# Gate and up blocks by seven products: 19 of 22 instead of 10, two of the weight sums made by adding transfers, the feed-forward in three parts

## The chip, the cores and the metric

The kernel runs on one core of a Trainium2 chip. The metric is the device time of one execution in microseconds; for a run of several executions it is the median. The core has a matrix engine (PE, whose weight loads are listed as PEld), a vector engine (DVE), an activation engine (ACT), a general engine (POOL) and a sequencer that mostly issues transfers (SP). Each works through its own queue in order, and they wait for each other by semaphores. DMA engines move data between main memory and the on-chip memory; matmul results stand in the banks of PSUM.

## The reference

Two layers of an encoder over 512 positions of width 1024, in float32. Each layer mixes three branches (attention, convolution, neighbourhood attention), then comes the part that matters here, the feed-forward with 2816 hidden channels, and then a gated input embedding:

```python
h = rmsnorm(x, norm_ffn[i])
x = x + (jax.nn.silu(h @ w_ffn_gate[i]) * (h @ w_ffn_up[i])) @ w_ffn_down[i]
h = rmsnorm(x, norm_ple[i])
x = x + jax.nn.sigmoid(h @ w_ple_gate[i]) * (p[i] @ w_ple_in[i])
```

`w_ffn_gate` and `w_ffn_up` are 1024 x 2816, `w_ffn_down` is 2816 x 1024.

## The kernel before

**Tiles.** Channels lie along the 128 partitions and the 512 positions along the free dimension. x is eight tiles of 128 x 512 (`x[0]` to `x[7]`), the hidden channels are 22 blocks of 128 (`NFB`). float32 precision comes from three matmuls per product (`mm3`, L174): each operand is split into a high half, which PE takes at its rounded precision, and a low half that holds the rest, and high x high, high x low and low x high are added. `split` (L161) makes the halves: ACT copies the high one (L142), DVE subtracts it for the low one (L156). `weights` (L165) loads a block of weights of up to 1024 columns into `wr` by a transfer from SP (L170) and splits it into `wh` and `wl`; there are three buffers of each. It does so under a raised priority, up to `w_ahead` = 400 steps ahead of the place where the products stand.

**Order.** PE's order is the program's order (`manual_schedule`); for the other engines a scheduler places the instructions by priority and dependency, and each then runs its queue in that order.

**Feed-forward (`ffn`, L1012).** The hidden blocks are worked in two halves of eleven (`HB`). For each block the products with gate and up are made, giving a tile g = silu(gate) * up, whose halves stand in `md`; after eleven blocks the down products follow: eight output tiles, each a sum over eleven blocks, whose weights come as 1024 and 384 columns. The result is multiplied by the norm's row factor `rb` and added to x (L1055, L1056).

**Plain blocks** make gate and up by `gemm`: eight chunks of the width by three matmuls of 512 columns each, twice, 48 matmuls.

**Blocks by seven products** (`SEVEN`, L52: ten of the 22, every second from 3 on; `seven`, L938) treat gate and up together as a 2 x 2 arrangement of blocks. The weights are a11, a12 (gate, first and second half of the width) and a21, a22 (up); the activations are b11, b12, b21, b22 (halves of the width by halves of the positions). Instead of eight block products there are seven of sums of the blocks (Strassen and Winograd's scheme): four of weights (s1 to s4) and four of activations (t1 to t4, made once per layer by `quarters`, L909). Each block product is four chunks by three matmuls of 256 columns, so 84 matmuls of half the width. Per block SP loads gate and up (two loads of 512 KB, L944, L945), DVE makes s1 to s4 (L960 to L964, into a `qk` buffer of 2048 columns, of which there are two), and ACT and DVE split [a11 a12], a22, [s1 s3] and [s2 s4]. The products go to three banks A, C and Q; three intermediate results are copied out by ACT (p1, p4, p5; L985 to L989) before more is added in the same place, and DVE joins the results by seven operations of 256 columns (L995 to L1001). Then silu (ACT), times up (DVE), and the split into `md`.

Two consecutive seven-product blocks would use different banks by the count `n`; with every second block plain they use `sc`, `sc`, `av`, and the plain ones `mm`.

The norms of `main_norm` (L247) take two short PE steps and a power on POOL (L221) and run beside the first products of the stage that follows; `pair` (L193) makes two outputs at once, all chunks but the last for both and then the last for both, so that the last activation may come late.

Of the kernel before, what the change touches and what calls it, by code (L numbers as in the profile page):

```python
# [12 lines left out]
F32R = mybir.dt.float32r  # L13
# [23 lines left out]
PLE = 256  # L37
DFF = 2816
NFB = DFF // P
HB = NFB // 2  # L40
EPS = 1e-6
OFF_QA, OFF_KA, OFF_VA, OFF_GLU = 0, 512, 1024, 1536
OFF_QC, OFF_KC, OFF_VC, OFF_G = 2560, 3072, 3584, 4096
# [5 lines left out]
BG = dict(glu=2, natten=1, values=3, diff=1, gatec=2, branchc=2, gateb=4, mergea=4, mergea2=2)  # L49
FIRST = (["v"] * 4 + ["pt"] * 2 + ["y", "b"], ["y"] * 5 + ["pt"] * 2 + ["b"])  # L50
EARLY = 6
SEVEN = (3, 5, 7, 9, 11, 13, 15, 17, 19, 21)  # L52
GAP = 144
BACC = dict(dynamic_dma_scratch_size=1024)

# [5 lines left out]
class Net:  # L61
# [131 lines left out]
    def pair(self, outs, aps, acts):  # L193


        ws = [self.weights(ap, 1024) for ap in aps]
        n = len(acts)
        for ks in (range(n - 1), (n - 1,)):
            for out, (wh, wl) in zip(outs, ws):
                for k in ks:  # L200
                    s = slice(k * P, (k + 1) * P)
                    self.mm3(out, wh[:, s], wl[:, s], *self.halves(acts[k]), k == 0, k == n - 1)
                    self.chunk()
# [705 lines left out]
    def quarters(self, x, h, j):  # L909


        one, two = slice(0, 256), slice(256, 512)
        g = lambda k: self.par(self.i, "ffn", k)
        f = []
        for k in (j, j + 4):
            v = self.sb("t", [P, 512])
            self.act(v, x[k], AF.Copy, scale=g(k))
            f.append(v)
        b11, b12, b21, b22 = f[0][:, one], f[0][:, two], f[1][:, one], f[1][:, two]
        u = self.sb("t", [P, 2, 256])  # L920
# [12 lines left out]
        ha, hb = self.halves(h[j]), self.halves(h[j + 4])  # L933
        cut = lambda p, c: (p[0][:, c], p[1][:, c])
        return dict(b11=cut(ha, one), b21=cut(hb, one), b22=cut(hb, two),
                    **{f"t{n + 1}": (o[:, 0], o[:, 1]) for n, o in enumerate(d)})

    def seven(self, wg, wu, bs, n):  # L938


        nc = self.nc
        with self.tc.high_priority(offset=min(self.w_ahead, self.tc.cur_priority - self.p0)):
            g, u = self.sb("wr", [P, 1024]), self.sb("wr", [P, 1024])
            nc.sync.dma_start(g, wg)  # L944
            nc.sync.dma_start(u, wu)  # L945
# [12 lines left out]
            s = self.sb("qk", [P, 2048])  # L958
            s1, s3, s2, s4 = (s[:, q * 512:q * 512 + 512] for q in range(4))
            self.tt(s1, a21, a22, ALU.add)  # L960
            self.tt(s3, a11, a21, ALU.subtract)
            halve(*wide(), s[:, :1024], ("s1", "s3"))
            self.tt(s2, s1, a11, ALU.subtract)
            self.tt(s4, a12, s2, ALU.subtract)  # L964
            halve(*wide(), s[:, 1024:], ("s2", "s4"))
        tags = ("mm", "mm", "mm") if n % 2 else ("sc", "sc", "av")
        A, C, Q = (self.ps(t, (P, 2, 256)) for t in tags)

        def product(out, w, b, first):
            wh, wl = ws[w]  # L970
            mm = nc.tensor.matmul
            for k in range(4):
                c = slice(k * P, k * P + P)
                bh, bl = bs[k][b]
                mm(out, wh[:, c], bh, start=first and k == 0, stop=False, skip_group_check=True)  # L975
# [19 lines left out]
        self.tt(p5, p5, p4, ALU.subtract)  # L995
        self.tt(gg[:, 0], A[:, 0], rb[:, 0], ALU.mult)
        self.tt(p1, p1, A[:, 1], ALU.add)
        self.tt(uu[:, 0], p1, Q[:, 0], ALU.add)
        self.tt(uu[:, 1], uu[:, 0], p5, ALU.add)
        self.tt(gg[:, 1], p1, C[:, 0], ALU.add)  # L1000
# [11 lines left out]
    def ffn(self, h, x):  # L1012
        self.phase = "ffn"
        i = self.i
        self.halfs, count = 0, 0
        st, hn, bs = [], [], self.four
        for half in range(2):
            mids = []
            for f in range(HB):
                fb = half * HB + f  # L1020
                md = self.sb((["z"] * 5 + ["y"] * 5 + ["pt"])[f], [P, 2, 512], F32R)
                mids.append(md)
                wg, wu = self.a["w_fg"][i, fb], self.a["w_fu"][i, fb]
                if fb in SEVEN:
                    count = (count + 1) % 2 if fb - 1 in SEVEN else 0
                    g = self.seven(wg, wu, bs, count)
                    self.split(md[:, 0, :], md[:, 1, :], g)
                    continue
                g = self.sb("t", [P, 512])
                pg, pu = self.ps("mm"), self.ps("mm")  # L1030
# [12 lines left out]

                def up(pu=pu, g=g, md=md):
                    self.tt(g, g, pu, ALU.mult)
                    self.split(md[:, 0, :], md[:, 1, :], g)

                self.ready(up)
                if fb in (0, 1):
                    self.four.append(self.quarters(x, h, 2 + fb))  # L1050
            for m in range(KD):
                ps = self.ps("mm")
                self.gemm(ps, self.a["w_fd"][i, half, m], mids)
                d = self.sb("t", [P, 512])
                self.tt(d, ps, self.rb, ALU.mult)  # L1055
                self.tt(x[m], x[m], d, ALU.add)  # L1056
                if half:
                    if m in (0, 2):
                        two = self.parts_of("qk", [2, 512], 2, F32R)
                    hn.append(self.norm_chunk(m, x[m], self.par(i, "ple", m),  # L1060
                                              two[m % 2] if m < 4 else "v", st))
        self.main_norm(st[0])
        return hn

# [256 lines left out]
def _layout(v):  # L1321
# [4 lines left out]
    for i in range(L):  # L1326
# [7 lines left out]
    down = f["w_ffn_down"].reshape(L, 2, HB * P, D)  # L1334
    return {
        "xT": np.ascontiguousarray(f["x"][0][n].T).reshape(KD, P, S),
        "pT": np.ascontiguousarray(f["p"][:, 0][:, n].transpose(0, 2, 1)).reshape(L, 2, P, S),
# [15 lines left out]
        "w_fd": _blocks(down),  # L1353
        "w_pi": _blocks(f["w_ple_in"]),
        "w_pg": _blocks(f["w_ple_gate"]),
    }
# [15 lines left out]
```

## Time and profile before

| | |
|---|---|
| median of 3 runs | 1801.97 us (1801.7 to 1802.68) |
| the profiled execution | 1802.28 us, of which 1800.3 us are the span from its first to its last instruction |
| PE busy | 1790.7 us (99%), 9346 matmuls |
| PEld busy | 1535.5 us (85%) |
| DVE busy | 1315.5 us (73%) |
| ACT busy | 846.9 us (47%) |
| POOL busy | 24.6 us (1%) |
| moved by DMA | 221.30 MB, a mean of 123 GB/s |
| mean granted PE clock | 0.999 |

How to read the lines: in the page, a group of instructions stands as line, engine, operation, output<-inputs, shapes and count, then busy time, the mean of one in ns, the idle time of the engine just before them and who ended it. In a timeline a row is start, duration (both in us), engine, line, operation, tiles. Start to start of two rows in a row is the pitch; durations overlap, since the engines begin an instruction before the previous one has written its last result. A row of DMA issues ends with the size in KB and the median time in us from issue to landing. L numbers of the profile are those of the kernel before.

### The profile page before, as it was taken

To read this page: it belongs to the slowest core of one execution; us is meant where nothing else is said; L and a number is where in the kernel's file an instruction comes from. 1 tells how busy PE (TensorE), PEld (TensorE's weight loads), DVE (VectorE), ACT (ScalarE), POOL (GpSimd) and SP (SyncE) were. 2 spreads that over 40 slices of the span, in tenths; PEclk is the share of its full clock that TensorE was granted. 3 is DMA by queue.
4 is the path that set the end of the run, shared out by engine and by line. 5 is a ranking of instruction groups with operands and counts; after the bars stand their busy time and mean duration, and the time that the engine had idled before them with its cause. 6 is when DMAs were issued, how large, how long until landed. Compare 5 with 4: busy or idle time off the path is not lost.

```text
span 1800.3 us, 25007 instructions
## 1 busy us (share of the span) xinstructions
PE 1790.7 (99%) x9346; PEld 1535.5 (85%) x9346; DVE 1315.5 (73%) x2198; ACT 846.9 (47%) x1457; POOL 24.6 (1%) x58
## 2 busy tenths in 40 slices
PE   9999999999999999999999999999999999999998
PEld 7888888888889889988888888888888898899887
DVE  7877888987767547665776788889886764577556
ACT  5577545325454324444535765552355543244444
POOL 0000000000000000000000000000000000000000
PEclk9999999999999999999999999999999999999999
DMA  5665531334423232233446655322253232333332
GB/s 205 193 179 167 159 111 54 103 105 148 142 83 110 84 123 94 94 110 126 143 140 202 169 160 149 98 76 96 92 192 112 96 104 75 101 110 102 103 115 94
DMA packets 90313, 221.30 MB, mean 123 GB/s; under 512 B 11984, under 2 KB 20688, under 8 KB 90192
## 3 DMA queue, kind: packets, MB, share of 16 engines
q1 hardware_dynamic: 89472, 218.39, 38.6%
q8 instruction: 74, 1.21, 0.3%
q10 hardware_dynamic: 720, 1.31, 0.2%
q14 instruction: 47, 0.39, 0.1%
HBM read 180.86 MB, written 7.34 MB: 105 GB/s over the span
## 4 chain that ended last, share of the span: by engine, by line
PE 96%; ACT 1%; DVE 1%; issue 0%; DMA 0%; POOLq 0%; DVEq 0%; ACTq 0%
PE ffn_mm L176 9%; PE ffn_mm L178 9%; PE ffn_mm L177 9%; PE ffn_sc L977 3%; PE ffn_sc L976 3%; PE ffn_sc L975 3%; PE mergea_mm L176 2%; PE mergea_mm L178 2%; PE mergea_mm L177 2%; PE diff_sc L783 2%; PE gatec_mm L176 2%; PE gatec_mm L177 2%; PE gatec_mm L178 2%; PE gateb_mm L178 2%; PE gateb_mm L177 2%; PE gateb_mm L176 2%
## 5 line engine op out<-in xcount | busy, mean ns | idle before, releaser
L142 ACT ACTIVATE ffn_wh<-ffn_wr 128x1024 fp32r<-128x1024 f32 (+1 forms) x132 | 122.7, 931 | 233.0 <-PE ffn_mm L177 126.2
L156 DVE TENSOR_TENSOR ffn_wl<-ffn_wr,ffn_wh 128x1024 fp32r<-128x1024 f32 (+1 forms) x132 | 139.7, 1061 | 119.7 <-ACT ffn_wh L142 119.7
L159 DVE SCALAR_TENSOR_TENSOR conv_z<-glu_z,pre_par,conv_z 128x512 f32<-128x512 f32 x240 | 179.7, 749 | 3.3
L176 PE MATMUL ffn_mm<-wo_h,ffn_wh 128*128 128x512 f32 x384 | 150.0, 391 | 0.0
L177 PE MATMUL ffn_mm<-wo_h,ffn_wh 128*128 128x512 f32 x384 | 149.6, 390 | 0.0
L178 PE MATMUL ffn_mm<-wo_h,ffn_wl 128*128 128x512 f32 x384 | 149.5, 389 | 0.0
L178 PEld LDWEIGHTS ffn_mm<-wo_h,ffn_wl 128*128 128x128 f32 x384 | 72.1, 188 | 15.2
L176 PEld LDWEIGHTS ffn_mm<-wo_h,ffn_wh 128*128 128x128 f32 x384 | 72.2, 188 | 14.3
L177 PEld LDWEIGHTS ffn_mm<-wo_h,ffn_wh 128*128 128x128 f32 x384 | 72.2, 188 | 14.2
L142 ACT ACTIVATE mergea_wh<-mergea_wr 128x1024 fp32r<-128x1024 f32 (+1 forms) x32 | 27.1, 846 | 96.8 <-PE mergea_mm L177 79.6
L142 ACT ACTIVATE ffn_wh<-ffn_qk 128x1024 fp32r<-128x1024 f32 x40 | 42.1, 1053 | 59.9 <-PE ffn_mm L177 59.9
L977 PE MATMUL ffn_sc<-wo_h,ffn_wl 128*128 128x256 f32 x240 | 67.9, 283 | 0.0
L976 PE MATMUL ffn_sc<-wo_h,ffn_wh 128*128 128x256 f32 x240 | 67.9, 283 | 0.0
L975 PE MATMUL ffn_sc<-wo_h,ffn_wh 128*128 128x256 f32 x240 | 67.8, 283 | 0.0
L176 PE MATMUL ffn_mm<-ffn_z,ffn_wh 128*128 128x512 f32 x160 | 62.3, 389 | 0.0
L177 PE MATMUL ffn_mm<-ffn_z,ffn_wh 128*128 128x512 f32 x160 | 62.3, 389 | 0.0
L178 PE MATMUL ffn_mm<-ffn_z,ffn_wl 128*128 128x512 f32 x160 | 62.2, 389 | 0.0
L176 PE MATMUL ffn_mm<-ffn_y,ffn_wh 128*128 128x512 f32 x160 | 62.2, 389 | 0.0
L177 PE MATMUL ffn_mm<-ffn_y,ffn_wh 128*128 128x512 f32 x160 | 62.2, 389 | 0.0
L178 PE MATMUL ffn_mm<-ffn_y,ffn_wl 128*128 128x512 f32 x160 | 62.2, 389 | 0.0
L156 DVE TENSOR_TENSOR ffn_t<-ffn_mm,wo_r 128x512 f32<-128x512 f32 x56 | 38.6, 689 | 29.3 <-PE ffn_mm L178 29.2
L142 ACT ACTIVATE ffn_t<-ffn_t 128x512 f32<-128x512 f32 x44 | 27.6, 626 | 59.3 <-DVE ffn_t L156 59.0
(727 smaller groups left out, 5502.4 us busy)
## 6 DMA issues: line engine op xcount, KB each, us to landing
ffn_wr<-w_fg SPq DMA_DIRECT2D x44, 512.0 KB, 4.5
ffn_wr<-w_fu SPq DMA_DIRECT2D x44, 512.0 KB, 3.5
ffn_wr<-w_fd SPq DMA_DIRECT2D x32, 512.0 KB, 3.4
natten_wr<-w_in SPq DMA_DIRECT2D x16, 512.0 KB, 4.2
natten_b<-bias SPq DMA_DIRECT2D x32, 256.0 KB, 3.9
diff_wr<-w_in SPq DMA_DIRECT2D x16, 512.0 KB, 3.9
gatec_wr<-w_in SPq DMA_DIRECT2D x16, 512.0 KB, 3.9
gateb_wr<-w_in SPq DMA_DIRECT2D x16, 512.0 KB, 3.5
```

Of the source, the lines that this page charges most:

```text
L142: i = self.nc.scalar.activation(out, in_, func, **kw)
L156: return self.nc.vector.tensor_tensor(out, a, b, op)
L159: return self.nc.vector.scalar_tensor_tensor(out, a, s, b, op0, op1)
L176: mm(out, wh, ah, start=first, stop=False)
L177: mm(out, wh, al, start=False, stop=False)
L178: mm(out, wl, ah, start=False, stop=last)
L783: self.nc.tensor.matmul(out, st4[:, u, qs], st[:, ks], start=n == 0, stop=n == 1)
L975: mm(out, wh[:, c], bh, start=first and k == 0, stop=False, skip_group_check=True)
L976: mm(out, wh[:, c], bl, start=False, stop=False, skip_group_check=True)
L977: mm(out, wl[:, c], bh, start=False, stop=k == 3, skip_group_check=True)
```

## The change

- `SEVEN` is 3 to 21: nineteen of the 22 blocks. Plain ones are 0, 1 and 2.
- The feed-forward is worked in three parts of eight, seven and seven blocks (`PARTS`), each followed by its down products over its blocks, so x is added to three times. The down weights are no longer cut in halves on the host; a part takes its columns (1024, 896, 896). The first two down products of each part are made by `pair`.
- The scheme's signs are turned so that all weight sums are additions: s1 = a11 + a21, s2 = a22 + a21, s3 = s1 + a22, s4 = s3 + a12. s1 and s2 are made without DVE: SP loads a11 and a22 into the `qk` buffer, and POOL issues two transfers that add a21 from main memory to them (`accum_op`). a22 has a load of its own into `r`. So SP issues four loads per block (256, 256, 512 and 256 KB) and POOL two of 256 KB. DVE makes s3 and s4 only.
- The split of [s3 s4] has its own two pairs of buffers, `y` for even and `pt` for odd blocks, and `wh`/`wl` serve [a11 a12] and [s1 s2]. The result tiles `md` stand in `z` and three of `y`.
- Banks alternate by the number of the block: even ones (the plain ones too) use `mm`, odd ones `sc`, `sc`, `av`.
- silu, the product with up and the split of a block are put off (`pending`) until the next block's p5 has been copied (`flush`), and `behind` orders an instruction after another without a wait; at the start of the second and third part s3 of the first two blocks is ordered behind the last result's split.

```diff
-HB = NFB // 2
+PARTS = (range(0, 8), range(8, 15), range(15, 22))
-SEVEN = (3, 5, 7, 9, 11, 13, 15, 17, 19, 21)
+SEVEN = tuple(range(3, 22))
@@ pair
-        ws = [self.weights(ap, 1024) for ap in aps]
+        ws = [self.weights(ap, n * P) for ap in aps]
@@ quarters
-        self.tt(t1, b12, b11, ALU.subtract)
-        self.tt(t2, b22, t1, ALU.subtract)
+        self.tt(t1, b11, b12, ALU.subtract)
+        self.tt(t2, b22, t1, ALU.add)
         self.tt(t3, b22, b12, ALU.subtract)
-        self.tt(t4, b21, t2, ALU.subtract)
+        self.tt(t4, t2, b21, ALU.subtract)
@@ seven
-    def seven(self, wg, wu, bs, n):
+    def seven(self, wg, wu, bs, tags, spare, md, first):
-            g, u = self.sb("wr", [P, 1024]), self.sb("wr", [P, 1024])
+            lo, up = slice(0, 512), slice(512, 1024)
+            g, a22 = self.sb("wr", [P, 1024]), self.sb("r", [P, 512])
+            s = self.sb("qk", [P, 2048])
+            s1, s2, s3, s4 = (s[:, q * 512:q * 512 + 512] for q in range(4))
+            nc.sync.dma_start(s1, wg[:, lo])
+            nc.sync.dma_start(s2, wu[:, up])
             nc.sync.dma_start(g, wg)
-            nc.sync.dma_start(u, wu)
-            a11, a12, a21, a22 = g[:, :512], g[:, 512:], u[:, :512], u[:, 512:]
+            nc.sync.dma_start(a22, wu[:, up])
+            for q in (s1, s2):
+                nc.gpsimd.dma_start(q, wu[:, lo], accum_op=ALU.add)
...
             halve(self.sb("kh", [P, 512], F32R), self.sb("a", [P, 512], F32R), a22, ("a22",))
-            s = self.sb("qk", [P, 2048])
-            s1, s3, s2, s4 = (s[:, q * 512:q * 512 + 512] for q in range(4))
-            self.tt(s1, a21, a22, ALU.add)
-            self.tt(s3, a11, a21, ALU.subtract)
-            halve(*wide(), s[:, :1024], ("s1", "s3"))
-            self.tt(s2, s1, a11, ALU.subtract)
-            self.tt(s4, a12, s2, ALU.subtract)
-            halve(*wide(), s[:, 1024:], ("s2", "s4"))
-        tags = ("mm", "mm", "mm") if n % 2 else ("sc", "sc", "av")
+            halve(*wide(), s[:, :1024], ("s1", "s2"))
+            i = self.tt(s3, s1, a22, ALU.add)
+            if first:
+                self.behind(i, self.held)
+            self.tt(s4, s3, g[:, up], ALU.add)
+            halve(*spare, s[:, 1024:], ("s3", "s4"))
...
-        product(C[:, 0], "s1", "t1", True)
-        self.act(p5, C[:, 0], AF.Copy)
+        product(C[:, 0], "s2", "t1", True)
+        self.flush(self.act(p5, C[:, 0], AF.Copy))
         product(A[:, 0], "a12", "b21", False)
-        product(Q[:, 0], "s3", "t3", False)
-        product(A[:, 1], "s2", "t2", True)
+        product(Q[:, 0], "s1", "t3", False)
+        product(A[:, 1], "s3", "t2", True)
         product(C[:, 0], "s4", "b22", False)
...
-        self.act(gg, gg, AF.Silu, table="silu")
-        self.tt(gg, gg, uu, ALU.mult)
-        return gg.rearrange("p a b -> p (a b)")
+        def rest(then):
+            i = self.act(gg, gg, AF.Silu, table="silu")
+            if then is not None:
+                self.behind(i, then)
+            self.tt(gg, gg, uu, ALU.mult)
+            self.held = self.split(md[:, 0, :], md[:, 1, :], gg.rearrange("p a b -> p (a b)"))
+        self.pending.append(rest)
+    def behind(self, i, then):
+        self.tc.add_manual_dep(
+            i.ins, then.ins.name,
+            mybir.DependencyInfo(mybir.DependencyClass.NoSync, mybir.DependencyReason.DATA),
+            reason="order",
+        )
+    def flush(self, then=None):
+        while self.pending:
+            self.pending.pop(0)(then)
@@ ffn
-        for half in range(2):
+        spare = [[self.sb(t, [P, 1024], F32R) for _ in range(2)] for t in ("y", "pt")]
+        for part in PARTS:
             mids = []
-            for f in range(HB):
-                fb = half * HB + f
-                md = self.sb((["z"] * 5 + ["y"] * 5 + ["pt"])[f], [P, 2, 512], F32R)
+            for f, fb in enumerate(part):
+                tags = (("mm", "mm", "mm"), ("sc", "sc", "av"))[fb % 2]
+                md = self.sb("z" if f < 5 else "y", [P, 2, 512], F32R)
...
-                    count = (count + 1) % 2 if fb - 1 in SEVEN else 0
-                    g = self.seven(wg, wu, bs, count)
-                    self.split(md[:, 0, :], md[:, 1, :], g)
+                    self.seven(wg, wu, bs, tags, spare[fb % 2], md, part[0] and f < 2)
                     continue
...
+            self.flush()
+            down = [self.a["w_fd"][i, m][:, part[0] * P:(part[-1] + 1) * P] for m in range(KD)]
+            two = [self.ps(("mm", "sc")[fb % 2 == 0]) for _ in range(2)]
+            self.pair(two, down[:2], mids)
             for m in range(KD):
-                ps = self.ps("mm")
-                self.gemm(ps, self.a["w_fd"][i, half, m], mids)
+                if m < 2:
+                    ps = two[m]
+                else:
+                    ps = self.ps("mm")
+                    self.gemm(ps, down[m], mids)
...
-                if half:
+                if part is PARTS[-1]:
```

More of the change, by code (lines that the diff above doesn't have):

```diff
@@ L987, in seven @@
         self.act(p4, Q[:, 0], AF.Copy)
-        product(C[:, 0], "s1", "t1", True)
-        self.act(p5, C[:, 0], AF.Copy)
+        product(C[:, 0], "s2", "t1", True)
+        self.flush(self.act(p5, C[:, 0], AF.Copy))
         product(A[:, 0], "a12", "b21", False)
-        product(Q[:, 0], "s3", "t3", False)
-        product(A[:, 1], "s2", "t2", True)
+        product(Q[:, 0], "s1", "t3", False)
+        product(A[:, 1], "s3", "t2", True)
         product(C[:, 0], "s4", "b22", False)
         rb = self.rb.rearrange("p (a b) -> p a b", a=2)
-        self.tt(p5, p5, p4, ALU.subtract)
+        self.tt(p5, p4, p5, ALU.subtract)
         self.tt(gg[:, 0], A[:, 0], rb[:, 0], ALU.mult)
-        self.tt(p1, p1, A[:, 1], ALU.add)
-        self.tt(uu[:, 0], p1, Q[:, 0], ALU.add)
+        self.tt(p1, A[:, 1], p1, ALU.subtract)
+        self.tt(uu[:, 0], p1, Q[:, 0], ALU.subtract)
         self.tt(uu[:, 1], uu[:, 0], p5, ALU.add)
-        self.tt(gg[:, 1], p1, C[:, 0], ALU.add)
+        self.tt(gg[:, 1], C[:, 0], p1, ALU.subtract)
         self.tt(gg[:, 1], gg[:, 1], rb[:, 1], ALU.mult)
-        self.act(gg, gg, AF.Silu, table="silu")
-        self.tt(gg, gg, uu, ALU.mult)
-        return gg.rearrange("p a b -> p (a b)")
+        def rest(then):
[14 more added lines that the diff above has]
+            self.pending.pop(0)(then)
     def chunk2(self):
@@ L1014, in ffn @@
         i = self.i
-        self.halfs, count = 0, 0
+        self.halfs, self.pending = 0, []
         st, hn, bs = [], [], self.four
-        for half in range(2):
+        spare = [[self.sb(t, [P, 1024], F32R) for _ in range(2)] for t in ("y", "pt")]
+        for part in PARTS:
             mids = []
-            for f in range(HB):
-                fb = half * HB + f
-                md = self.sb((["z"] * 5 + ["y"] * 5 + ["pt"])[f], [P, 2, 512], F32R)
+            for f, fb in enumerate(part):
+                tags = (("mm", "mm", "mm"), ("sc", "sc", "av"))[fb % 2]
+                md = self.sb("z" if f < 5 else "y", [P, 2, 512], F32R)
                 mids.append(md)
@@ L1024, in ffn @@
                 if fb in SEVEN:
-                    count = (count + 1) % 2 if fb - 1 in SEVEN else 0
-                    g = self.seven(wg, wu, bs, count)
-                    self.split(md[:, 0, :], md[:, 1, :], g)
+                    self.seven(wg, wu, bs, tags, spare[fb % 2], md, part[0] and f < 2)
                     continue
                 g = self.sb("t", [P, 512])
-                pg, pu = self.ps("mm"), self.ps("mm")
+                pg, pu = (self.ps(t) for t in tags[:2])
                 if fb == 0:
@@ L1050, in ffn @@
                     self.four.append(self.quarters(x, h, 2 + fb))
+            self.flush()
+            down = [self.a["w_fd"][i, m][:, part[0] * P:(part[-1] + 1) * P] for m in range(KD)]
+            two = [self.ps(("mm", "sc")[fb % 2 == 0]) for _ in range(2)]
+            self.pair(two, down[:2], mids)
             for m in range(KD):
[L1052 to L1053 removed]
+                if m < 2:
[3 more added lines that the diff above has]
+                    self.gemm(ps, down[m], mids)
                 d = self.sb("t", [P, 512])
@@ L1056, in ffn @@
                 self.tt(x[m], x[m], d, ALU.add)
-                if half:
+                if part is PARTS[-1]:
                     if m in (0, 2):
-                        two = self.parts_of("qk", [2, 512], 2, F32R)
+                        qk = self.parts_of("qk", [2, 512], 2, F32R)
                     hn.append(self.norm_chunk(m, x[m], self.par(i, "ple", m),
-                                              two[m % 2] if m < 4 else "v", st))
+                                              qk[m % 2] if m < 4 else "v", st))
         self.main_norm(st[0])
@@ L1333, in _layout @@
     w_0 = _first(w_in[0])
-    down = f["w_ffn_down"].reshape(L, 2, HB * P, D)
     return {
@@ L1352, in _layout @@
         "w_fu": _blocks(f["w_ffn_up"]),
-        "w_fd": _blocks(down),
+        "w_fd": _blocks(f["w_ffn_down"]),
         "w_pi": _blocks(f["w_ple_in"]),
```

## The prediction

> **What bounds the kernel now.** I read the page first: busy shares, slices, chain.
>
> ```profile
> span 1800.3 us, 25007 instructions
> ...
> PE 1790.7 (99%) x9346; PEld 1535.5 (85%) x9346; DVE 1315.5 (73%) x2198; ACT 846.9 (47%) x1457; POOL 24.6 (1%) x58
> ...
> PE   9999999999999999999999999999999999999998
> ...
> PEclk9999999999999999999999999999999999999999
> ...
> PE 96%; ACT 1%; DVE 1%; issue 0%; DMA 0%; POOLq 0%; DVEq 0%; ACTq 0%
> ```
>
> TensorE works 1790.7 of 1800.3 us at full clock, and the chain that ended last is 96% PE. Then the stretches of the feed-forward, the only place that the change touches (columns: PE, PEld, DVE, ACT, POOL busy, clock, DMA share, GB/s):
>
> ```profile
> 550.00:600.00 50.00, 50.00 (x324) 45.83 (x323) 32.18 (x49) 21.07 (x31) 0.00 (x0) 1.00 0.26 87
> ...
> 700.00:800.00 100.00, 100.00 (x625) 90.71 (x624) 68.09 (x104) 43.40 (x62) 0.00 (x0) 1.00 0.33 104
> ```
>
> PE has no gap, DVE is at 64 to 68%, DMA at a third. So only fewer or shorter matmuls help here, and they help in full until another engine or a transfer makes PE wait.
>
> **What one more block by seven products saves.** From the timeline of PE: the first matmul of a seven-product block, of the plain block after it, and of the next two.
>
> ```profile
> 531.28 0.28 PE L975 MATMUL ffn_sc<-wo_h,ffn_wh 128*128 128x256 f32 x1
> ...
> 541.35 0.40 PE L176 MATMUL ffn_mm<-wo_h,ffn_wh 128*128 128x512 f32 x1
> ...
> 552.26 0.28 PE L975 MATMUL ffn_sc<-wo_h,ffn_wh 128*128 128x256 f32 x1
> ...
> 562.33 0.40 PE L176 MATMUL ffn_mm<-wo_h,ffn_wh 128*128 128x512 f32 x1
> ```
>
> A seven-product block (84 matmuls of 256 columns) takes 541.35 - 531.28 = 10.07 us, 0.12 each; a plain one (48 of 512 columns) 552.26 - 541.35 = 10.91. The listed durations (0.28, 0.40) overlap, so pitches count. The change converts nine blocks in each of two layers: 18 x (10.91 - 10.07) = 15.1 us off PE, the only gain. The down products keep their 22 x 8 x 3 matmuls per layer.
>
> **DVE in a run of seven-product blocks.** Before, plain and seven-product blocks alternate; now five, seven and seven stand in a row. DVE's pitches, one row of each width and its successor:
>
> ```profile
> 542.29 0.42 DVE L156 TENSOR_TENSOR ffn_t<-ffn_t,ffn_a 128x256 f32<-128x256 f32 x1
> 542.62 1.22 DVE L156 TENSOR_TENSOR ffn_wl<-ffn_wr,ffn_wh 128x1024 fp32r<-128x1024 f32 x1
> 543.76 0.69 DVE L156 TENSOR_TENSOR ffn_a<-ffn_wr,ffn_kh 128x512 fp32r<-128x512 f32 x1
> 544.36 0.69 DVE L156 TENSOR_TENSOR ffn_qk<-ffn_wr 128x512 f32<-128x512 f32 x1
> 544.96 0.69 DVE L156 TENSOR_TENSOR ffn_qk<-ffn_wr,ffn_wr 128x512 f32<-128x512 f32 x1
> ```
>
> 256 columns 0.33, 1024 columns 1.14, 512 columns 0.60 us. A new block gives DVE three low halves of 1024 (g, s1s2, s3s4), five operations of 512 (low a22, s3, s4, gate x up, low half of the result) and seven of 256: 3.42 + 3.00 + 2.31 = 8.7 us, of PE's 10.07: 87%. With all four sums left on DVE it would be 9.9. So DVE's throughput holds, but its cover shrinks from a third of the time to 1.3 us a block.
>
> **The two sums by transfers.** s1 and s2 now come from an SP load (256 KB) and, when that has landed, a POOL transfer that adds the other 256 KB. Per block SP issues four loads where it issued two (0.33 us each), POOL two. Both must be done before DVE adds a22 to s1 (s3; the first suffices) and ACT splits s1s2. The trace has no POOL transfer at all:
>
> ```profile
> q1 hardware_dynamic: 89472, 218.39, 38.6%
> q8 instruction: 74, 1.21, 0.3%
> q10 hardware_dynamic: 720, 1.31, 0.2%
> q14 instruction: 47, 0.39, 0.1%
> ...
> ffn_wr<-w_fu SPq DMA_DIRECT2D x44, 512.0 KB, 3.5
> ...
> mergea_wr<-w_br_a SPq DMA_DIRECT2D x16, 256.0 KB, 2.5
> ...
> pre_x<-xT SPq DMA_DIRECT2D x7, 256.0 KB, 5.0
> ...
> diff_r<-rope SPq DMA_DIRECT2D x4, 256.0 KB, 5.4
> ```
>
> So call the time of an adding transfer, from its load's landing to its own, L2. From below 2.5 us, a plain load of 256 KB in a quiet queue; nothing suggests that adding is faster. From above 5.4, 256 KB in a crowded one. It must also read what it adds to, so its nearest row is the 512 KB load, 3.5; for POOL's own work and the next block's load of g that runs beside it I put 0.5 on top: L2 = 4.0.
>
> What it costs depends on a loop. In the changed program DVE stands in this order (block 11 on PE): s3 and s4 of block 13, low a22 of 12, p5 of 11, gate x up of 10, low half of s1s2 of 12. There are two buffers of sums: the load for block n+2 is issued when DVE has read s1s2 of block n for the last time. SP follows DVE at once:
>
> ```profile
> 538.25 1.23 DVE L156 TENSOR_TENSOR ffn_wl<-ffn_wr,ffn_wh 128x1024 fp32r<-128x1024 f32 x1 [1.62 <-ACT ffn_wh L142]
> ...
> 539.51 0.33 SPq L945 DMA_DIRECT2D ffn_wr<-w_fu  x1
> ```
>
> (539.48 to 539.51). One turn, from s1s2 of a block to s1s2 of the next: load 2.5 + L2 + DVE's six operations 4 x 0.60 + 0.33 + 1.22 = 3.95 + 0.1 for handing over = 6.55 + L2. A turn of more than 10.07 makes DVE later by L2 - 3.5 in each block. What is in front: s1s2 may be split when the running block's a12 product (its fourth of 12 matmuls, 5.76 us in) has freed a weight buffer.
>
> ```profile
> 548.11 0.61 ACT L142 ACTIVATE ffn_t<-ffn_t 128x512 f32<-128x512 f32 x1
> 548.63 0.62 ACT L142 ACTIVATE ffn_z<-ffn_t 128x512 fp32r<-128x512 f32 x1
> 552.29 1.06 ACT L142 ACTIVATE ffn_wh<-ffn_qk 128x1024 fp32r<-128x1024 f32 x1 [3.05 <-PE ffn_mm L177]
> ...
> 553.89 0.39 ACT L142 ACTIVATE ffn_t<-ffn_sc 128x256 f32<-128x256 f32 x1
> ```
>
> ACT follows a product's end by 0.19 (552.26 + 1.44 = 553.70 to 553.89): 5.95 + 1.06 + 1.22 and 0.05 for handing over = 8.3 us into the block. PE needs it as the third product of the next, 10.07 + 2.88 less the weight load = 12.7. Slack 4.4 us. (ACT itself has 3 x 1.06 + 3 x 0.62 + 3 x 0.39 = 6.2 us a block and is no bound.) In a run of seven, five turns add up (the first two blocks are prepared during the down products), in a run of five, three. PE's loss is 4 x max(0, 5x - 4.4) + 2 x max(0, 3x - 4.4) with x = L2 - 3.5. At L2 = 4.0, x = 0.5: 2.5 us of 4.4 is used and PE loses nothing. The loss begins at L2 = 4.4, and at 5.1 (4 x 3.6 + 0.8 = 15.2) it has eaten the gain.
>
> Here the Trainium skill speaks against such transfers twice. Its page "DMA: Bandwidth & Descriptors" (Anatomy of one DMA) fits a POOL transfer as 2.0 us plus bytes over 436 GB/s, an estimated 2.6 for 256 KB, with about 1 us to the first byte where SP's needs 0.6 (its Specifications); "Collectives: The Full Stack" (The bandwidth ceiling) says that an add is slow because it "needs two source reads", an estimated 0.6 more. By these L2 would be 3.2 to 4.2, and the sum is the same as mine; no run here shows a POOL transfer yet.
>
> **Three parts instead of two.** Eight more times per layer a down product is multiplied and added to x: 16 x 2 x 0.60 = 19 us of DVE, against splits of 1024 + 384 columns twice that become 1024 + 896 + 896.
>
> ```profile
> L156 DVE TENSOR_TENSOR wo_x<-wo_x,ffn_t 128x512 f32<-128x512 f32 x32 | 22.1, 692 | 1.1
> ...
> L156 DVE TENSOR_TENSOR ffn_wl<-ffn_wr,ffn_wh 128x384 fp32r<-128x384 f32 x32 | 17.8, 557 | 73.3 <-ACT ffn_wh L142 73.3
> ```
>
> A down product of eight or seven chunks takes PE 24 or 21 matmuls of 0.227 us (10.91 / 48), 5.4 or 4.8 us, while DVE has about 1.1 + 1.2 = 2.3 (3.5 in the last part, with the norm's two): hidden, zero. Its end: the last block's result needs three DVE operations of 256 (1.0), then silu, gate x up and both halves (0.61 + 0.69 + 0.62 + 0.69), each handed over in about 0.2: some 4.6 us after its last product. The first two down products now take turns, seven or six chunks each before the last chunk is asked for: 2 x 6 x 0.68 = 8.2 us of cover at least. Zero; without that turn-taking 6 x 0.68 = 4.1 would leave under 1 us, four times. The banks of PSUM alternate by block, so that a block finds its three read out a whole block earlier; zero.
>
> **What moves in the queues.** The silu, product and split of a block stand after the third copy of the next, and the fence on s3 only orders DVE. Blocks 3 and 4 load their sums during w_o: on SP the first stands ahead of w_o's fifth load and waits for merge_b's end. w_o is eight products of 24 matmuls, 5.4 us each, so that fifth weight is used 4 x 5.4 = 22 us later, and behind it nothing is due sooner; on POOL four transfers stand ahead of the power of the norm, which comes after all eight, 43 us later. Zero for both. Signs in the quarters change no count.
>
> **Sum.** The profiled execution took 1802.28 us by the clock (span 1800.3), the median is 1801.97: 0.3 apart, so I count from the median. 1801.97 - 15.1 = 1786.9; 1787.
>
> **Rivals.** *The loop decides, slower (0.21).* L2 above 5.1. At 5.4, the upper row, x = 1.9: 4 x 5.1 + 2 x 1.3 = 23 lost, 1810; DVE would show waits for DMA ahead of s3 and PE gaps at the third product, from the fourth or fifth block of a run on. For it: no POOL transfer in the trace, a load of g in flight beside, two adding transfers behind each other on POOL. Against it: the quiet rows, 2.5 and 3.5, are what SP's loads in this stretch show (DMA share 0.26 to 0.33).
>
> *The loop bites, but less than the gain (0.17).* L2 from 4.4 to 5.1; at 4.8, x = 1.3, 4 x 2.1 = 8.4 lost: 1795. About 0.05 of the whole lies within 0.2% of before (3.6 us, about what a measurement of this kernel can tell from no change).
>
> *DVE holds up POOL.* If POOL could not prepare a transfer while DVE runs an operation on the port that they share, each would wait for up to one operation, 1.22: L2 = 5.2 and 1803, no faster than before. Its chance is in the two above, a few in a hundred. The Trainium skill's page "SBUF — State Buffer" (two separate sides) has this trap for DVE copies; by its own section Who interferes with whom, tensor_tensor does not stall these transfers, and by that rule this rival falls. Every DVE operation quoted above is a TENSOR_TENSOR; no run here shows it either way.
>
> *The change does not do what it says:* nothing in the trace speaks for it, since before already has such blocks at 10.07.
>
> **How the numbers follow.** Full gain 0.62, at 1787. The range goes from 1785.5 (PE's bound less the 1 us by which the runs differ, 1801.7 to 1802.68) to 1806 (x = 1.75), which leaves out slow cases of about 0.15; for the full gain alone it is 1785.5 to 1790. Faster by over 0.2%: 0.62 + 0.17 - 0.05 = 0.74. Within: 0.05. Slower: 0.21.
>
> **What would show it.** PE at 100% in both feed-forwards, seven-product blocks every 10.07 us in a row; 38 blocks' L975 to L977 rows; a software queue with 76 transfers of 256 KB landing within 4.4 us; DVE 85 to 90% busy there; DVE's waits for the adding transfers at s3 up to 2 us with no wait of PE behind them. The prediction is wrong if PE waits for ffn_wl at the third product, growing along a run, or if ACT's copy of the second product stands behind a late a22.

## The result, and the profile after

The changed kernel takes 1808.57 us (median of 7 runs, 1805.7 to 1810.93), the kernel before in the same comparison 1802.3 (1801.7 to 1802.68): a ratio of 1.0034 with a 95% interval of 1.0024 to 1.0043. It is slower by 6 us where 15 less were predicted. The profiled execution took 1805.7 us, the fastest of the seven, so the profile shows the loss at its smallest.

The page of the changed kernel, first its span, busy times, queues and chain, then the groups and DMA issues that are new:

```profile
span 1803.9 us, 26909 instructions
...
PE 1783.7 (99%) x9994; PEld 1556.3 (86%) x9994; DVE 1391.5 (77%) x2354; ACT 879.5 (49%) x1531; POOL 92.2 (5%) x134
...
q0 software_dynamic: 10944, 19.93, 7.2%
...
PE 82%; DVE 8%; DMA 5%; ACT 3%; issue 2%; SPq 0%; POOLq 0%; DVEq 0%; ACTq 0%
...
L952 POOL DMA_DIRECT2D ffn_qk<-w_fu x76 | 67.5, 1003 | 596.6 <-DVE ffn_t L156 364.7
...
L156 DVE TENSOR_TENSOR ffn_qk<-ffn_qk,ffn_r 128x512 f32<-128x512 f32 x38 | 25.9, 690 | 77.1 <-DMA ffn_qk<-w_fu 77.1
...
ffn_qk<-w_fu POOLq DMA_DIRECT2D x76, 256.0 KB, 5.5
...
ffn_qk<-w_fg SPq DMA_DIRECT2D x38, 256.0 KB, 2.6
```

PE is busy 7 us less, with more but shorter matmuls, but the chain that ended last is PE for 82% instead of 96%: 8% are DVE and 5% the adding transfers. DVE stood 77.1 us in front of s3 (`ffn_qk<-ffn_qk,ffn_r`) waiting for them; an adding transfer takes 5.5 us from issue to landing where SP's load of as many bytes takes 2.6. The 5.5 is the median over both transfers of a block; the first, for which s3 waits, is taken by itself below.

The time lies in the runs of seven-product blocks. First and last matmul of blocks 8 to 14 of the first layer, from the timeline of PE in the changed kernel:

```profile
625.50 0.28 PE L978 MATMUL ffn_mm<-wo_h,ffn_wh 128*128 128x256 f32 x1
...
699.73 0.28 PE L980 MATMUL ffn_mm<-wo_h,ffn_y 128*128 128x256 f32 x1
```

That is 699.85 - 625.50 = 74.35 us with the last pitch of 0.12, where seven blocks of 10.07 make 70.49: 3.86 lost. The other runs of seven lost 3.71, 3.90 and 5.70, the runs of five 0.49 and 0.46; 18.1 in all, against 15.1 gained. The down products take 119.77 us a layer (119.74 before). So 3.0 of the profiled 3.6 us of longer span come from there. The rest lies between the layers; 0.6 of it are two waits of PE in the neighbourhood attention (L708 on ACT, 1.4 us instead of 0.8), whose cause stays open.

Inside a run the loss comes late. One turn in the timeline of the changed kernel, while blocks 12 and 13 are on PE (rows of DVE, ACT, SP, POOL and PE; the bracket is the idle time before the instruction and what ended it):

```profile
666.02 0.69 DVE L156 TENSOR_TENSOR ffn_qk<-ffn_qk,ffn_r 128x512 f32<-128x512 f32 x1 [2.59 <-DMA ffn_qk<-w_fu]
...
667.35 0.68 DVE L156 TENSOR_TENSOR ffn_a<-ffn_r,ffn_kh 128x512 fp32r<-128x512 f32 x1
...
668.09 0.39 PE L980 MATMUL ffn_mm<-wo_e,ffn_a 128*128 128x256 f32 x1 [0.22 <-DVE ffn_a L156]
...
668.89 1.22 DVE L156 TENSOR_TENSOR ffn_wl<-ffn_qk,ffn_wh 128x1024 fp32r<-128x1024 f32 x1
669.00 0.63 ACT L142 ACTIVATE ffn_z<-ffn_t 128x512 fp32r<-128x512 f32 x1 [3.97 <-DVE ffn_t L156]
...
670.13 0.33 SPq L947 DMA_DIRECT2D ffn_qk<-w_fg  x1
...
670.16 0.39 PE L980 MATMUL ffn_mm<-wo_rp,ffn_wl 128*128 128x256 f32 x1 [0.38 <-DVE ffn_wl L156]
...
671.44 0.36 ACT L142 ACTIVATE ffn_t<-ffn_mm 128x256 f32<-128x256 f32 x1
...
671.85 0.39 PE L978 MATMUL ffn_mm<-wo_h,ffn_wh 128*128 128x256 f32 x1 [0.23 <-ACT ffn_t L142]
...
673.51 1.79 POOL L952 DMA_DIRECT2D ffn_qk<-w_fu  x2 [10.28 <-DVE ffn_t L156]
...
678.08 0.69 DVE L156 TENSOR_TENSOR ffn_qk<-ffn_qk,ffn_r 128x512 f32<-128x512 f32 x1 [2.98 <-DMA ffn_qk<-w_fu]
```

DVE's wait at s3 (666.02) holds back what is behind it: the low half of a22, for which PE waits in its second product (668.09), and the low half of s1s2, for which it waits in the third (670.16); ACT's copy of the first product (671.44) stands behind three high halves, the first of which, a result's, waited 3.97 us for DVE (669.00), and holds the fourth, which adds to the same bank (671.85). The load for the block after next is issued when the low half of s1s2 is done (670.13), POOL's transfer 3.38 later, and s3 of that block can go 4.57 after that (678.08). The turn is 678.08 - 666.02 = 12.06 us. PE needs one in 10.07.

### The profile page after: what moved, and what is told of

The parts are those of the page before. It is cut to its first block, busy times and chain, and to the rows that moved or that the text cites. A ratio compares the mean times of both kernels' runs of the same rounds, so it can differ in the third digit from the quotient of the medians.

```text
span 1803.9 us, 26909 instructions
## 1 busy us (share of the span) xinstructions
PE 1783.7 (99%) x9994; PEld 1556.3 (86%) x9994; DVE 1391.5 (77%) x2354; ACT 879.5 (49%) x1531; POOL 92.2 (5%) x134
## 3 DMA queue, kind: packets, MB, share of 16 engines
HBM read 210.74 MB, written 7.34 MB: 121 GB/s over the span
## 4 chain that ended last, share of the span: by engine, by line
PE 82%; DVE 8%; DMA 5%; ACT 3%; issue 2%; SPq 0%; POOLq 0%; DVEq 0%; ACTq 0%
PE ffn_mm L178 5%; PE ffn_mm L177 5%; PE ffn_mm L176 5%; DMA ffn_qk<-w_fu 5%; PE mergea_mm L177 2%; PE mergea_mm L178 2%; PE mergea_mm L176 2%; PE diff_sc L783 2%; PE gatec_mm L176 2%; PE gatec_mm L177 2%; PE gatec_mm L178 2%; PE gateb_mm L177 2%; PE gateb_mm L178 2%; PE wo_mm L177 2%; PE gateb_mm L176 2%
## 5 line engine op out<-in xcount | busy, mean ns | idle before, releaser
L156 DVE TENSOR_TENSOR ffn_wl<-ffn_wr,ffn_wh 128x1024 fp32r<-128x1024 f32 (+1 forms) x98 | 114.6, 1176 | 15.3 <-ACT ffn_wh L142 14.4
L952 POOL DMA_DIRECT2D ffn_qk<-w_fu x76 | 67.5, 1003 | 596.6 <-DVE ffn_t L156 364.7
L156 DVE TENSOR_TENSOR ffn_t<-ffn_mm,wo_r 128x512 f32<-128x512 f32 (+1 forms) x66 | 40.5, 614 | 59.4 <-PE ffn_mm L178 59.4
L176 PE MATMUL ffn_mm<-ffn_z,ffn_wh 128*128 128x512 f32 x220 | 85.6, 389 | 0.0
L177 PE MATMUL ffn_mm<-ffn_z,ffn_wh 128*128 128x512 f32 x220 | 85.6, 389 | 0.0
L156 DVE TENSOR_TENSOR ffn_qk<-ffn_qk,ffn_r 128x512 f32<-128x512 f32 x38 | 25.9, 690 | 77.1 <-DMA ffn_qk<-w_fu 77.1
L178 PEld LDWEIGHTS ffn_mm<-ffn_z,ffn_wl 128*128 128x128 f32 x220 | 41.3, 188 | 8.6
L176 PEld LDWEIGHTS ffn_mm<-ffn_z,ffn_wh 128*128 128x128 f32 x220 | 41.3, 188 | 8.5
L177 PEld LDWEIGHTS ffn_mm<-ffn_z,ffn_wh 128*128 128x128 f32 x220 | 41.3, 188 | 8.5
L156 DVE TENSOR_TENSOR ffn_wl<-ffn_qk,ffn_wh 128x1024 fp32r<-128x1024 f32 x38 | 46.3, 1219 | 1.3 <-ACT ffn_wh L142 0.6
L978 PE MATMUL ffn_sc<-wo_h,ffn_wh 128*128 128x256 f32 x160 | 46.0, 287 | 1.0 <-ACT ffn_t L142 1.0
L142 ACT ACTIVATE natten_wh<-natten_wr 128x1024 fp32r<-128x1024 f32 x24 | 25.4, 1058 | 41.4 <-issue 15.2
L979 PE MATMUL ffn_sc<-wo_h,ffn_wh 128*128 128x256 f32 x160 | 45.2, 283 | 0.0
```

Of the source, the lines that this page charges most:

```text
L142: i = self.nc.scalar.activation(out, in_, func, **kw)
L156: return self.nc.vector.tensor_tensor(out, a, b, op)
L176: mm(out, wh, ah, start=first, stop=False)
L177: mm(out, wh, al, start=False, stop=False)
L178: mm(out, wl, ah, start=False, stop=last)
L952: nc.gpsimd.dma_start(q, wu[:, lo], accum_op=ALU.add)
```

## The experiments

Theory A: the loop through DVE's order and the two buffers of sums sets the time, by the turn of 12 us. Theory B: the adding transfers cost by themselves, through contention or POOL's work. Theory C: DVE is too full for these blocks. Every ratio is to the kernel before, run beside.

**DVE's order (label order).** s3 of a block goes behind the low half of s1s2 of the block before it (`halve` returns that instruction of DVE here).

```diff
-            halve(*wide(), s[:, :1024], ("s1", "s2"))
+            low = halve(*wide(), s[:, :1024], ("s1", "s2"))
             i = self.tt(s3, s1, a22, ALU.add)
             if first:
                 self.behind(i, self.held)
+            elif self.low7 is not None:
+                self.behind(i, self.low7)
+            self.low7 = low
```

> The changed kernel with one more ordering on DVE: the sums s3 of block n+2 stand behind the low half of s1s2 of block n+1 instead of ahead of it. All transfers, loads and operations stay. Theory A (the loop): in the changed kernel one turn is low half of s1s2, load, adding transfer, s3, low half of s1s2 of the next block, 11.2 to 12.6 us by the trace, against 10.07 of PE; with the order exchanged the turn spans two blocks (20.1 us for about 12), PE's stalls of 18.1 us vanish but for a few tenths, 1787 to 1789. Theory B (the transfers cost as such, by contention with weight loads or by work on POOL, whatever stands behind them): 1805 to 1810 as before the exchange. Theory C (DVE is simply full at 8.7 of 10.07 us): 1800 to 1810, because what is moved forward pushes something else back.

1788.75 us (1788.39 to 1789.54), ratio 0.9926 (0.9913 to 0.9938): faster than both kernels. The windows of its run of blocks 8 to 14 (columns: PE, PEld, DVE, ACT, POOL busy, clock, DMA share, GB/s), and in the fence behind it those of the same run in the changed kernel:

```profile
625.00:695.00 70.00, 70.00 (x585) 70.00 (x584) 57.68 (x95) 38.24 (x60) 12.41 (x14) 1.00 0.72 172
```

```profile
625.00:700.00 75.00, 72.94 (x592) 71.44 (x592) 57.93 (x96) 37.07 (x60) 12.38 (x14) 1.00 0.67 162
```

DVE does the same 58 us of work, POOL the same 12.4, in 70 us instead of 75, and PE has no gap. The turn is still there, but s3 no longer waits (timeline of this kernel):

```profile
652.11 1.22 DVE L156 TENSOR_TENSOR ffn_wl<-ffn_qk,ffn_wh 128x1024 fp32r<-128x1024 f32 x1 [0.83 <-ACT ffn_wh L142]
653.26 0.68 DVE L156 TENSOR_TENSOR ffn_qk<-ffn_qk,ffn_r 128x512 f32<-128x512 f32 x1
653.37 0.33 SPq L947 DMA_DIRECT2D ffn_qk<-w_fg  x1
...
656.42 1.76 POOL L952 DMA_DIRECT2D ffn_qk<-w_fu  x2 [8.06 <-DMA ffn_qk<-w_fg]
...
663.34 0.68 DVE L156 TENSOR_TENSOR ffn_qk<-ffn_qk,ffn_r 128x512 f32<-128x512 f32 x1
```

The load of 653.37 now serves the s3 of 663.34, and that stands behind a low half of s1s2 whose own sums were loaded a block earlier. The adding transfers are no faster (5.6 us median in this kernel). B and C fall as causes of the loss: they had given 1805 to 1810 and 1800 to 1810.

**Another way out of the loop (label three).** DVE's order as in the changed kernel; the same two buffers are shared out as three places for s1s2 and one for s3s4.

```diff
+        self.sums = [t for _ in range(2) for t in self.parts_of("qk", [1024], 2)]
...
-            s = self.sb("qk", [P, 2048])
-            s1, s2, s3, s4 = (s[:, q * 512:q * 512 + 512] for q in range(4))
+            s12, s34 = self.sums[n % 3], self.sums[3]
+            s1, s2, s3, s4 = (s[:, q:q + 512] for s in (s12, s34) for q in (0, 512))
```

> The changed kernel with the same two buffers of sums shared out differently: three places for s1s2 in turn and one for s3s4. DVE's order stays as in the changed kernel (s3 of block n+2 ahead of the low half of s1s2 of block n+1), all transfers and operations stay; only, the load of s1 and s2 may go a block earlier. Theory A: the turn needs both the order and the late load, so this opens it as well as exchanging the order did: 1787 to 1790, and DVE's waits for the adding transfers fall from 77.1 us to less than 20. If it is the order on DVE alone that costs (s3 in the wrong place, whatever the load does): 1800 to 1810.

1788.77 us (1788.52 to 1789.15), ratio 0.9925 (0.9907 to 0.9943), the same as the other order. DVE's waits for the adding transfers, 77.1 us before, are no longer among its waits. The chain on its page:

```profile
PE 94%; DVE 2%; ACT 2%; DMA 1%; issue 1%; SPq 0%; POOLq 0%; DVEq 0%; ACTq 0%
```

So the order alone does no harm, nor does the long transfer alone: it takes the early s3 and the late load together. (The s3 of a block stands ahead of the low half of s1s2 of the block before here too, at 658.27 and 662.55 us.)

**A longer turn (labels swap and swap2).** First only the two adding transfers were exchanged in the program:

```diff
-            for q in (s1, s2):
+            for q in (s2, s1):
```

> The changed kernel with the two adding transfers exchanged: s2's is issued first, s1's second. In the changed kernel's trace the second lands 1.3 to 1.8 us after the first, and s3 on DVE needs s1. Theory A (the loop): each turn grows by about 1.6 us; over the four turns that stall in each of the four runs of seven and the two in each run of five that is 4 x 4 x 1.6 + 2 x 2 x 1.6 = 32 us more, 1835 to 1845. Theories B and C: the same transfers and the same work on DVE, 1805 to 1811.

1807.56 us (1805.09 to 1808.62), ratio 1.0029 (1.0019 to 1.0038). The scheduler set the two back in the order of their loads, every queue stayed as it was, and the run is only a second measurement of the changed kernel; it says nothing between the theories. With the loads exchanged too, s1 is really second:

```diff
-            nc.sync.dma_start(s1, wg[:, lo])
             nc.sync.dma_start(s2, wu[:, up])
+            nc.sync.dma_start(s1, wg[:, lo])
...
-            for q in (s1, s2):
+            for q in (s2, s1):
```

> The changed kernel with the loads of s1 and s2 exchanged as well as their adding transfers, so that the one that s3 waits for is really the second on SP and on POOL (exchanging the adding transfers alone left every queue as it was). Theory A (the loop through s3): by the changed kernel's trace the second adding transfer lands 1.5 to 1.9 us after the first, so each turn goes from about 12.0 to 13.7 us; 4 x 4 x 1.7 + 2 x 2 x 1.7 = 34 us more, and up to 48 if the first turn of each run slips too: 1842 to 1856. Theory B (transfers cost as such) and theory C (DVE full): the same work everywhere, 1805 to 1811.

1856.16 us (1852.65 to 1861.85), ratio 1.0307 (1.0288 to 1.0326). The median turn in the last four blocks of the runs of seven went from 11.92 to 13.39 us with the same work on every engine. Its waits of DVE and PE:

```profile
DVE ffn_qk L156 <- DMA ffn_qk<-w_fu: 130.6, 26, 6.7
...
PE ffn_av L980 <- DVE ffn_a L156: 16.1, 9, 3.6
PE ffn_mm L980 <- DVE ffn_a L156: 15.4, 10, 1.8
```

As A expected, and neither B nor C did. It is at the upper end of the range given. In the profiled execution one stall also lowered the clock, to 0.50 for 3.4 us (last section), which can account for under 2 us.

**Transfers that do not add (label plain).**

```diff
-                nc.gpsimd.dma_start(q, wu[:, lo], accum_op=ALU.add)
+                nc.gpsimd.dma_start(q, wu[:, lo])
```

> The changed kernel with the 76 POOL transfers made plain ones: they overwrite s1 and s2 with a21 instead of adding it, so the sums are not the reference's; same queue, same bytes from memory, same waits. Theory A: L2 (first load's landing to the first transfer's landing, 4.5 to 5.9 us now) falls if it is the adding that takes long: at L2 of 3.5 or less no stall is left, 1787 to 1789; if the queue of POOL is as slow without adding, the time stays at 1805 to 1810, and A stands with another reason for its size. Theory B: 1805 to 1810, since the traffic stays.

1793.15 us (1791.25 to 1793.44), ratio 0.9947 (0.9933 to 0.996): between the two answers. From the issue and the landing of each transfer in the two traces (medians over the last four blocks of the four runs of seven), the first transfer takes 4.64 us with adding and 3.95 without, the turn 11.92 and 11.25. Groups and issues of this kernel:

```profile
L952 POOL DMA_DIRECT2D ffn_qk<-w_fu x76 | 41.4, 544 | 605.4 <-DVE ffn_t L156 404.8
...
ffn_qk<-w_fu POOLq DMA_DIRECT2D x76, 256.0 KB, 3.8
```

So adding is 0.7 us of it at the median, and a POOL transfer without it is still 1.4 slower than the load (2.54); how much of that is other transfers under way beside it is worked out below. A turn of 11.25 still loses 3.7 us in the profiled runs of seven (72.17, 72.06, 70.55 and 70.84 us against 70.49).

**One transfer instead of two (label one_add).**

```diff
-            for q in (s1, s2):
+            for q in (s1,):
```

> The changed kernel without the second adding transfer: s2 stays a22 alone, so the result is not the reference's; s1's load, add and all waits behind it stay, 38 POOL transfers instead of 76. It asks whether the first adding transfer takes its 4.5 us because the second runs beside it. If so, its time from issue to landing falls towards the 2.5 to 3 us of a load and L2 towards 3.5: 1787 to 1793. If an adding transfer takes that long by itself, L2 stays at about 5 and the time at 1803 to 1810. Theory B: half of the excess of 18.1 goes, 1798.

1807.1 us (1804.93 to 1808.67), ratio 1.0025 (1.0015 to 1.0034). Half the adding transfers are gone, and the time is that of the changed kernel. The first takes as long alone, 4.63 us at the median (4.64 with the second beside it), and the turn is 11.94. On its page:

```profile
ffn_qk<-w_fu POOLq DMA_DIRECT2D x38, 256.0 KB, 4.6
```

The number of transfers costs nothing, the time of the one in the loop costs all. B falls a second time.

**No runs of blocks (label alternate).**

```diff
-SEVEN = tuple(range(3, 22))
+SEVEN = tuple(range(3, 22, 2))
```

> The changed kernel with seven products only in the ten odd blocks 3 to 21, as in the kernel before, all else as changed (sums by adding transfers, three parts, alternating banks). Theory A (the loop): a turn of 12 us has 20.98 us from one such block to the next, nothing stalls: 1801 to 1803.5, level with before; it also says whether the three parts cost anything. Theory B (each adding transfer costs as such, 18.1 us over 38 blocks, 0.48 each): 20 blocks x 0.48 = 9.5 over before, 1811. Theory C: 1801 to 1803.

1802.58 us (1802.34 to 1803.17), ratio 1.0002 (0.9992 to 1.0011): the three parts, the adding transfers and the alternating banks together are level with before, where B had given 1811. DVE still waits for adding transfers there, and none of PE's waits is behind them; all 20 blocks take 10.07 us.

```profile
DVE ffn_qk L156 <- DMA ffn_qk<-w_fu: 28.4, 12, 6.2
```

**One more block (label order_22).** The kernel with the exchanged order, and block 2 by seven products too (`SEVEN = tuple(range(2, 22))`).

> The kernel with the exchanged order on DVE, and block 2 of each layer by seven products too (20 of 22). PE: 2 x 0.84 = 1.7 us less than 1788.75, so 1787.0, if the fourth set of quarters, which is made after block 1, is ready for the second product of block 2, 2.9 us in. If its chain on ACT and DVE (scaling, four sums, four splits) is not, PE waits there for some us in each layer, 1790 to 1798.

1802.08 us (1800.47 to 1803.17), ratio 0.9999 (0.999 to 1.0008): the gain of the order is lost again in two places. PE's waits in this kernel:

```profile
PE ffn_mm L982 <- ACT ffn_v L142: 5.0, 2, 2.5
PE ffn_mm L983 <- DVE ffn_v L156: 3.9, 4, 1.6
```

Blocks 2 to 7 take 67.52 us where six blocks of 10.08 make 60.5: 7.0 lost in each layer. The fourth set of quarters (`ffn_v`) is not ready, as the second expectation said; a slower clock comes on top (last section), and the time lies above the 1790 to 1798 that it gave. With the quarters made where they are, the twentieth block costs about as much as the other conversions gained.

## Why the prediction was wrong, point by point

- *PE bounds the kernel; a converted block saves 0.84 us; 15.1 in all.* Right. Without the loop, in the kernel with the exchanged order, the feed-forwards are 14.7 us shorter (7.34 a layer); its 1788.75 is 1.7 above the predicted 1787, of which about 0.9 lies between the layers (0.6 of it the same two waits at L708; their cause stays open).
- *The adding transfer's L2 = 4.0 us.* This is the term that failed. It measured 5.31 (median of the last four blocks of the runs of seven, 4.58 to 6.95): 0.67 from the load's landing to POOL's issue, the same each time, and 4.64 to its landing. The two sizes that made it up were both too small. The first, "its nearest row is the 512 KB load, 3.5" stood for the adding transfer itself: of the first transfers of blocks 5 to 21 of the changed kernel, seven had at most 40 KB of other queues' data moving beside them, and they took 3.77 to 4.16 us, 4.00 at the median. The second, "0.5 on top", stood for POOL's own work and the load beside it: these measured 0.67 until POOL's issue and some 0.6 for the crowding (4.64 against 4.00). Ten transfers with 430 to 470 KB of other queues beside them took 4.35 to 4.80. So even in a quiet queue L2 is 0.67 + 4.00 = 4.67, above the 4.4 where the loss begins, and crowding takes it past 5.1.
  How much of the 4.00 is adding, the plain transfers show: with at most 16 KB beside them six took 2.66 to 2.99 us, 2.78 at the median, which is near a load of SP; the other 28, with 330 KB and more, took 3.17 to 4.87. Alone, then, adding costs about 1.2 us, and much of a plain transfer's 3.95 is crowding. (No run varies the crowding by itself; this split is read off the transfers as they fell.) One row each, a plain one alone (1624.24), an adding one alone (1518.45) and an adding one with 441 KB beside it (773.63):

```profile
ffn_qk<-w_fu POOLq DMA_DIRECT2D x1, 256.0 KB, 2.7
```

```profile
ffn_qk<-w_fu POOLq DMA_DIRECT2D x1, 256.0 KB, 4.0
```

```profile
ffn_qk<-w_fu POOLq DMA_DIRECT2D x1, 256.0 KB, 4.8
```

  The DMA share in a run rose from 0.33 to 0.67 with the change. The second adding transfer isn't what slows the first: without it the share was 0.53, and the first took as long. A window in the runs of the kernel with one transfer:

```profile
650.00:700.00 50.00, 47.14 (x378) 45.52 (x377) 39.34 (x67) 23.94 (x39) 3.93 (x5) 1.00 0.53 138
```

- *The loop: a turn of 6.55 + L2, slip x over 10.07, loss 4 x max(0, 5x - 4.4) + 2 x max(0, 3x - 4.4).* Right in mechanism, place and nearly in size. With the measured turns it gives these losses, beside those measured against the loop-free 1788.75: changed kernel, x = 1.85, 21.7 and 19.8; plain transfers, x = 1.18, 6.0 and 4.4; swap2, x = 3.32, 59.9 and 67.4 (under 2 us of it the clock's). Of the two signs named, the waits at the third product came, growing along a run; the late copy came too, but of the first product, behind the high half of a result, and the late a22 held PE directly, at the second product.
- *The rival "the loop decides, slower", 1810, chance 0.21.* This is what happened, at 1808.57. What stood against it, "the quiet rows, 2.5 and 3.5, are what SP's loads in this stretch show", was no argument: those loads don't add, and the share of 0.26 to 0.33 at which they were read became 0.67 by the change itself.
- *DVE's throughput holds.* Right: 57.68 us in 70 with all its work done (82%; 87% was reckoned).
- *Three parts, banks, queues at zero.* Right to within the measurement (alternate, 0.9992 to 1.0011), and with the exchanged order the runs of seven have no gap.
- *DVE holds up POOL.* Not seen. Two adding transfers of the changed kernel, from issue to landing (columns: DVE busy, clock, DMA share, GB/s): DVE worked through nearly all of the first and a third of the second, and they took as long.

```profile
685.36:689.90 4.54, 4.43 (x8) 1.00 0.87 172
673.51:678.06 4.55, 1.59 (x3) 1.00 0.88 184
```

  POOL's own time for a first transfer was 0.86 us with DVE at work throughout (637.79) and 0.87 with DVE idle (463.26). By the rule of the Trainium skill's page "SBUF — State Buffer" (Who interferes with whom) this rival fell, and the trace agrees. (The 1803 given for it leaves out the runs of five; by the formula it is 1804.7.)
- *What the Trainium skill would have given.* Its page "DMA: Bandwidth & Descriptors" (Anatomy of one DMA) makes an estimated 2.6 us for a POOL transfer of 256 KB; the plain ones with next to nothing beside them agree (2.66 to 2.99), those with other transfers in flight don't (3.95 at the median of a run's last blocks), and the measurement decides. The estimated 0.6 more for two source reads, from "Collectives: The Full Stack" (The bandwidth ceiling), is near the 0.7 between the medians of both kernels, and half of the 1.2 between the quiet transfers.

## What to carry to other kernels

When a transfer is put into a loop between engines, the loop's turn is to be compared with the time the bounding engine takes for a round, and a price known only from transfers of another kind and queue is no middle value: with break-even at 5.1 and the bounds at 2.5 and 5.4, the unknown was the whole decision. An in-order engine makes such loops when an instruction that waits for a late transfer stands ahead of one that releases the buffer of the next; moving that one instruction, or giving the buffer one place more, was worth 20 us here, and neither added nor removed any work. Such a wait at the head of DVE's queue was harmless where the turn had two rounds to itself: where blocks alternate, 28.4 us of waiting cost nothing.

## What the runs showed of the hardware

In the runs of seven blocks, a transfer of POOL's queue took 3.95 us for 256 KB where SP's took 2.54 (both medians), and 2.66 to 2.99 with next to nothing of other queues beside it; adding made it 4.64, and 3.77 to 4.16 with little beside it. POOL issued it 0.67 us after the landing it waited for, where SP follows the end of DVE's instruction in 0.02 (670.11 to 670.13). POOL is busy 0.54 us for a plain one, 0.89 for an adding one (medians; means 544 and 1003 ns).

The times of the changed kernel spread over 5.2 us, those of before over 1.0, those with the exchanged order over 1.2. The transfer in its loop varied from 3.91 to 6.29 us; that this is what spreads the time no run shows.

A stall can cost more than itself. PE's two waits at block 2 in the kernel with 20 blocks, and windows of PE around them (columns: PE busy, clock, DMA share, GB/s):

```profile
524.43 0.39 PE L983 MATMUL ffn_mm<-ffn_v,ffn_kh 128*128 128x256 f32 x1 [1.64 <-DVE ffn_v L156]
...
527.42 0.58 PE L982 MATMUL ffn_mm<-ffn_v,ffn_kh 128*128 128x256 f32 x1 [2.49 <-ACT ffn_v L142]
```

```profile
522.00:524.00 2.00, 0.79 (x7) 1.00 0.01 4
524.00:526.00 2.00, 0.50 (x2) 0.81 0.82 172
526.00:528.00 2.00, 0.58 (x1) 0.50 1.05 286
528.00:530.00 2.00, 1.69 (x8) 0.50 0.47 96
530.00:532.00 2.00, 2.00 (x11) 0.50 0.35 114
532.00:534.00 2.00, 2.00 (x19) 0.98 0.00 0
```

The waits were 1.64 and 2.49 us long with two matmuls between them, and the clock fell to 0.50 during the second: the row from 524 to 526 has a mean of 0.81 already. It stayed at 0.50 up to 532, for 4 us after the waits, in which PE did 8 and 11 matmuls in 2 us instead of 19. The stalls in the feed-forward of the changed kernel, up to 0.8 us of idle time each, never did this: its clock stayed at 1.00. Nor did one of 2.15 us in swap2 (PE idle up to 1586.74, clock 1.00), while one of 3.65 us there did, with a clock of 0.66 over the next 5 us (the fences below). The Trainium skill's page "TensorE: Matmul & The Clock Gate" (HAM oscillation — how this bites in real kernels) puts the limit at idle gaps of about 3.4 us. The two stalls of swap2 agree with that; the kernel with 20 blocks doesn't, since none of its waits was that long, and there the measurement decides.

```profile
669.87 0.39 PE L980 MATMUL ffn_av<-wo_e,ffn_a 128*128 128x256 f32 x1 [3.65 <-DVE ffn_a L156]
```

```profile
670.00:675.00 5.00, 4.97 (x28) 0.66 0.46 152
```
